# Corrections and outputs share one PSUM bank, state products take the other, and the work around them is spread: one layer of a hybrid attention and recurrence backbone

## The chip, the cores and the metric

The kernel runs on one core of a Trainium2 chip. A core has a matrix engine (TensorE, PE in the profile; PEld are its weight loads), a vector engine (VectorE, DVE), a scalar engine (ScalarE, ACT), GpSimd (POOL), a queue that issues transfers (SyncE, SP) and 16 DMA engines. Matmul results land in PSUM, which has 8 banks of 512 fp32 values in each of 128 partitions; DVE and ACT empty it. The metric is the time of one execution on the device, in microseconds; lower is better.

## The reference, cut to what matters

One layer works on 1024 latent tokens and 256 context tokens of width 1024. One input projection feeds 8 heads of differential attention and 16 heads of a recurrence that is run in both directions; both are gated and go through one output projection, and a norm ends it.

```python
def rwkv_scan(r, w, k, v, kk, b, s0, reverse):
    def step(S, inp):
        r_t, w_t, k_t, v_t, kk_t, b_t = inp
        sa = jnp.einsum('bhvk,bhk->bhv', S, -kk_t)
        S = S * w_t[:, :, None, :] + sa[..., None] * b_t[:, :, None, :] + v_t[..., None] * k_t[:, :, None, :]
        return S, jnp.einsum('bhvk,bhk->bhv', S, r_t)
    s_final, y = lax.scan(step, s0.astype(F32), xs, reverse=reverse)

def block(qblk):                                        # attention, 128 queries
    s = jnp.einsum('bqhmd,bkhmd->bhmqk', qblk, k).astype(F32) * scale
    p = jax.nn.softmax(s, axis=-1)
    a = p[:, :, 0] - lam * p[:, :, 1]
    return jnp.einsum('bhqk,bkhv->bqhv', a.astype(v.dtype), v)
```

After the scan the outputs of both directions are added, normed for each head, given a bonus and a gate, and projected together with the attention.

## The kernel before, in words

The first part of the kernel norms the tokens and makes all projections; it is not changed. For the recurrence, it cuts time into chunks of 32 steps and writes the operands of each chunk to DRAM: `ra` (receptance and removal keys) and `kt` (key rows, and the triangular products inside a chunk). A triangular 32x32 system has to be inverted for each chunk; `inverse` does this on GpSimd for a whole item at a time and writes the result to DRAM as `td`.

The second part, `mix_phase`, interleaves recurrence, attention, norms and output projection. The recurrence works on groups of four pairs of heads. An item is one group over 256 tokens (8 chunks); there are 10 items. A tick is one chunk of an item, with both directions and all 8 heads of the group at once, so there are 80 ticks. A part is two ticks (`HN`), and the operands `L` and `R` of a part lie in one of two slots, which `load_part` fills a part ahead. The four pairs are handled as two pair groups (`duos`, index `w`).

`step` writes the instructions of a tick in this order. Corrections: 32 small matmuls (line 893) give the part of the update that depends on the state. They are copied from PSUM into the rows 96 to 127 of `R` (line 901), for one pair group by ACT and for the other by DVE. In the second tick of a part, `prep` multiplies the next part's `L` with the inverse `Tb` (line 803) into the PSUM tile `yb`, and ACT copies that into `L` (line 806). State products: 32 matmuls (line 913) give the new state; DVE multiplies them with the decay of the chunk into the next `R` (line 924). Outputs: 32 matmuls (line 936), copied by ACT into the tile `ys` (line 939), which `store_y` writes to DRAM. Each pair group has a bank of PSUM of its own, `bank[w]`, in which corrections, outputs and state products of this pair group lie beside each other. The framework lets two engines on one bank follow the order of the text, also where they touch different columns.

Two calls of `fill` in a tick put other work into the text: pieces of `attention` by a credit in units of the kernel's own cost table (`RATES` and `total`), pieces of the inversion of the next item, and steps of the generators in `norms` and `projs`. Attention works on blocks of 128 queries: `scores` (line 1057 on PE, line 1060 on DVE, then the exponential on ACT, line 1068), `weight` and `combine` on DVE, `trans` (line 1089 on PE, line 1091 on ACT), `values` (line 1104). `norm` norms the recurrence's outputs of two pairs over 256 tokens; `load_wo` loads and splits the output weights into a high and a low part (`wst`, `wohi`, `wolo`).

The text's order is not yet the engines' order. A planner gives each instruction a priority by its place in the text and lays out for each engine, ahead of the run, a fixed sequence: at each point the ready instruction with the best priority, by the planner's own estimate of durations. `ahead(n)` moves the priority of a stretch of text `n` places forward; `HPC` is 500. On the chip each engine and SP's queue then take their instructions strictly in that sequence, each waiting for its own semaphores.

## Time and profile before

| what | value |
|---|---|
| runs, median of 3 | 2613.61 us (2607.57 to 2620.56) |
| profiled execution | 2612.43 us |
| its span, first to last instruction | 2610.6 us |
| mean granted clock of TensorE, share of full speed | 0.943 |
| projections | 0 to about 1240 us |
| recurrence with attention | about 1240 to 2390 us |
| tail | to the end |

The span is the time from the first to the last instruction of the profiled execution. An engine's busy time is the union of its instructions; matmuls are pipelined, so a busy PE need not be at its peak. The granted clock is the share of full speed that PE's clock was given. A wait is put down to the instruction that released it.

### The profile page before, as it was taken

The page shows a single profiled execution, that of the slowest core. Times are in us where ns is not written, and L with a number is a line of the kernel's source. Part 1 is how long each engine was busy: PE and PEld are TensorE (multiplying, and loading weights), DVE is VectorE, ACT ScalarE, POOL GpSimd, SP SyncE. Part 2 cuts the span into 40 slices and gives each one's busy share as a digit, 9 for nine tenths or more (in the row PEclk, how much of TensorE's full clock was granted, in tenths as well). Part 3 has the DMA queues.
Part 4 walks back from the last instruction along what each step waited for, and adds up shares of the span by engine and source line. Part 5 has one row for each costly group of instructions (what it writes and reads, how often), then busy time and mean ns, then how long its engine had stood idle before and what let it go on. Part 6 is the DMA issues. An engine that isn't in the chain of part 4 may idle for free.

```text
span 2610.6 us, 60873 instructions
## 1 busy us (share of the span) xinstructions
PE 2363.7 (91%) x23907; PEld 1902.6 (73%) x23907; DVE 1559.8 (60%) x3210; ACT 1192.9 (46%) x2606; POOL 1166.5 (45%) x1725
## 2 busy tenths in 40 slices
PE   6999999999999999898698989898989998898796
PEld 4888888888888888787466767676766676776674
DVE  5656565555455655533566877685745565576558
ACT  3334443334334343331466666574545554564342
POOL 4234343243433342465446666556647311043564
PEclk9999999999999999998799999897988998999898
DMA  7465656565646564567978887877887888787445
GB/s 240 108 157 134 178 143 181 139 164 161 155 128 161 135 180 120 165 167 165 225 156 166 163 163 146 165 150 169 167 200 183 211 191 190 176 222 207 148 146 181
DMA packets 516734, 437.56 MB, mean 168 GB/s; under 512 B 156552, under 2 KB 460852, under 8 KB 511329
## 3 DMA queue, kind: packets, MB, share of 16 engines
q1 hardware_dynamic: 514352, 427.94, 66.8%
q0 software_dynamic: 2096, 5.75, 1.2%
q8 instruction: 188, 3.08, 0.5%
q14 instruction: 98, 0.79, 0.1%
HBM read 258.69 MB, written 163.86 MB: 162 GB/s over the span
## 4 chain that ended last, share of the span: by engine, by line
PE 55%; DMA 19%; DVE 8%; POOL 6%; SPq 5%; issue 3%; ACT 2%; POOLq 0%; DVEq 0%; ACTq 0%
DMA L<-kt 5%; PE sc L1057 5%; PE po L1104 4%; PE bank L913 3%; PE pa L1089 3%; PE yb L803 3%; PE pg L449 3%; DMA acc<-acc 2%; PE pso L1298 2%; DMA wst<-w_out 2%; PE pso L1299 1%; DMA Tb<-td 1%; PE pso L1300 1%; PE bank L936 1%; PE psg_v L335 1%
## 5 line engine op out<-in xcount | busy, mean ns | idle before, releaser
L1057 PE MATMUL sc<-ka,q 128*128 128x512 f32 (+1 forms) x832 | 302.3, 452 | 17.5 <-DVE pb L1060 9.3
L1060 DVE TENSOR_SCALAR_CACHE_REDUCE pb<-sc,mn 128x512 f32<-128x512 f32 x256 | 191.6, 749 | 112.2 <-PE sc L1057 104.4
L1068 ACT ACTIVATE pb<-pb,mn 128x1536 f32<-128x1536 f32 (+1 forms) x160 | 218.4, 1365 | 75.3 <-DVE pb L1060 74.5
L734 POOL TENSOR_TENSOR tmp<-aw,tt 128x31 f32<-128x31 f32 (+15 forms) x310 | 163.4, 527 | 168.9 <-DMA aw<-kt 67.8
L1104 PE MATMUL po<-vk,aT 128*128 128x128 f32 x1600 | 237.2, 289 | 0.9 <-ACT aT L1091 0.7
L1104 PEld LDWEIGHTS po<-vk,aT 128*128 128x128 f32 x1600 | 217.2, 201 | 17.2 <-ACT aT L1091 1.4
L479 POOL TENSOR_SCALAR ta<-ta,ka 128x256 f32<-128x256 f32 x80 | 81.1, 1014 | 292.8 <-DVE bk L477 292.7
L456 ACT COPY km<-ptk 64x256 f32<-64x256 f32 x320 | 117.4, 367 | 182.3 <-PE ptk L453 160.4
L736 POOL TENSOR_TENSOR tt<-tt,tmp 128x31 f32<-128x31 f32 (+15 forms) x310 | 180.8, 583 | 18.2
L803 PE MATMUL yb<-L,Tb 32*32 32x96 f32 x2496 | 105.3, 269 | 81.1 <-DMA L<-kt 59.5
L806 ACT COPY L<-yb 32x384 f32<-32x384 f32 x312 | 146.3, 469 | 67.9 <-PE yb L803 63.8
L1057 PEld LDWEIGHTS sc<-ka,q 128*128 128x128 f32 x832 | 137.8, 201 | 53.6 <-DVE pb L1060 20.1
L1081 DVE SCALAR_TENSOR_TENSOR pb<-pb,cc,pb 128x512 f32<-128x512 f32 (+1 forms) x208 | 167.8, 856 | 2.0
L1091 ACT COPY aT<-pa 128x512 f32<-128x512 f32 (+1 forms) x208 | 116.2, 570 | 104.0 <-PE pa L1089 102.2
L924 DVE TENSOR_TENSOR R<-bank,wc 64x256 f32<-64x256 f32 x312 | 130.9, 420 | 54.6 <-PE bank L913 45.3
L450 DVE TENSOR_TENSOR km<-pg,msk 128x512 f32<-128x512 f32 x80 | 55.1, 688 | 175.7 <-PE pg L449 147.0
L1089 PE MATMUL pa<-ident,pb 128*128 128x128 f32 x800 | 137.7, 297 | 17.6 <-DVE acc L1292 10.4
L803 PEld LDWEIGHTS yb<-L,Tb 32*32 32x32 f32 x2496 | 66.3, 114 | 116.2 <-issue 42.2
L1060 DVE TENSOR_SCALAR_CACHE_REDUCE pb<-sc 128x512 f32<-128x512 f32 (+1 forms) x160 | 101.3, 636 | 80.7 <-PE sc L1057 67.8
L913 PEld LDWEIGHTS bank<-R,L 128*64 128x64 f32 x2560 | 102.2, 152 | 49.1 <-issue 20.5
L913 PE MATMUL bank<-R,L 128*64 128x64 f32 x2560 | 126.2, 244 | 8.3 <-ACT R L901 4.3
L1089 PEld LDWEIGHTS pa<-ident,pb 128*128 128x128 f32 x800 | 97.2, 150 | 45.1 <-DVE acc L1292 13.1
(354 smaller groups left out, 6496.2 us busy)
## 6 DMA issues: line engine op xcount, KB each, us to landing
kt<-km SPq DMA_DIRECT2D x160, 256.0 KB
L<-kt SPq DMA_DIRECT2D x80, 512.0 KB
acc<-acc SPq DMA_DIRECT2D x50, 512.0 KB
ra<-ra SPq DMA_DIRECT2D x160, 128.0 KB
L<-ra SPq DMA_DIRECT2D x80, 256.0 KB
R<-vb SPq DMA_DIRECT2D x160, 64.0 KB
y<-ys SPq DMA_DIRECT2D x80, 128.0 KB
yn<-y SPq DMA_DIRECT2D x40, 256.0 KB
```

The costliest lines, as they stand in the source:

```text
L734: e.tensor_tensor(mv, aw[:n, t, t + 1:CH].unsqueeze(2).broadcast_to([n, w, j]), tt[:n, t:t + 1, 0:j].broadcast_to([n, w, j]), op=ALU.mult)
L736: e.tensor_tensor(tt[:n, t + 1:CH, 0:j], tt[:n, t + 1:CH, 0:j], mv, op=ALU.add)
L803: nc.tensor.matmul(pp[32 * q:32 * q + 32, n:n + 96], Tb[96:128, e, HN * q + c, :], L[96:128, e, q // 2, q % 2, c, 0:96], start=True, stop= ...
L806: nc.scalar.copy(L[96:128, :, q // 2, q % 2, :, 0:96], pp[32 * q:32 * q + 32, 0:192 * HN].rearrange("p (e c y) -> p e c y", e=2, y=96))
L913: nc.tensor.matmul(bank[w][hv(h), o_:o_ + 64], L[:, e, h, d, k, 0:64], R[:, k, d, e, hv(h)], start=True, stop=True, tile_position=(0, 64 * h))
L924: nc.vector.tensor_tensor(dst[:, :, :, hv(h)], bank[w][hv(h), 256:512].rearrange("p (d e v) -> p d e v", e=2, d=2), wcs[p0][hv(h), 2 * w:2 ...
L1057: nc.tensor.matmul(sc, q[:, v, m, qc], ka[:, m, 0:kn], start=(v == 0), stop=(v == 1))
L1060: nc.vector.tensor_scalar(pm[:, c * 512:c * 512 + kn], sc, -0.125, mn[:, c - 1:c] if c else None, op0=ALU.mult, op1=ALU.min, accum_out=mn[ ...
L1068: nc.scalar.activation(v, v, AF.Exp, bias=mn[:, c:c + 1], scale=-1.0, accum_out=B["l"][:, m, B["b"]:B["b"] + 1])
L1081: nc.vector.scalar_tensor_tensor(a, B["p"][1][:, v], B["cc"], a, op0=ALU.mult, op1=ALU.add)
L1089: nc.tensor.transpose(pt[:, t * P:(t + 1) * P], B["p"][0][:, 512 * c + t * P:512 * c + (t + 1) * P], ident)
L1104: nc.tensor.matmul(po, B["aT"][c][:, t * P:(t + 1) * P], vk[:, t, :], start=(c == 0 and t == 0), stop=(c == last and t == nt - 1))
```

## The change

The two PSUM tiles change their roles. `bank[0]` takes the corrections (columns 0 to 255) and the outputs (256 to 511) of both pair groups, `bank[1]` their state products. The corrections are emptied in four copies of 32x256, all on ACT, for eight of 32x128 on two engines; the outputs in one copy for two. All of the tick from the corrections to the multiplies, the first `prep` included, is put ahead by 500 places (before, only copies and multiplies were); the outputs are put ahead by `HPY`, which is 0. An output tile holds two chunks for four, in two buffers for one, and is stored once a part.

The inversions run as one generator over all items. It is paced evenly at 33 steps for each 8 ticks and starts 4 ticks ahead (`INVA`), where before it ran at 8 steps a tick from the start of each item. In `norm`, one add and two subtracts go from GpSimd to DVE. In `attention`, exponentials are written one or two pieces later than their scores, `weight` and `combine` of a block move into the next block's text, one at a time, and the values stand between scores. The credit starts at minus two ticks (`LEAD`). `load_wo` issues two loads ahead of the split of the first.

```diff
--- before.py
+++ after.py
@@ -33,6 +33,8 @@
 CH = 32
 SEG = 256
 NC = SEG // CH
+INVA = 4
+LEAD = 2
 HN = 2
 NF = NC // HN
 NL = 4
@@ -45,7 +47,7 @@
 RATES = (1.06, 0.68)
 ES = 1
 TBUF = 1
-YBUF = 1
+YBUF = 2
 NDEL = 10
 ODEL = 14
 PDEL = 2
@@ -833,7 +835,7 @@
...
-    bank = [psx.tile([P, 512], F32, name=f"bank{w}") for w in duos]
+    bank = [psx.tile([P, 512], F32, name=f"bank{n}") for n in range(2)]
     yb = psx.tile([P, 512], F32, name="yb")
     sts, wcs = {}, {}
 
@@ -859,7 +861,7 @@
             nc.gpsimd.memset(R[0:64, 0], 0.0)
         if sg != 0:
             return
-        px = bank[w]
+        px = bank[1]
...
@@ -884,35 +886,34 @@
         c = HN * f + k
         p0, sg = items[m]
         hv = lambda h: slice(64 * h, 64 * h + 64)
-        for w in duos:
-            L, R = slots[w, j % 2]
+        later_prep = k == HN - 1 and j + 1 < n_part
+        with ahead(HPC):
             for d in range(2):
                 for e in range(2):
-                    for h in range(2):
-                        u = 64 * e + 32 * h
-                        nc.tensor.matmul(bank[w][u:u + 32, 64 * d:64 * d + 64], L[0:96, e, h, d, k, 96:128],
-                                         R[0:96, k, d, e, hv(h)], start=True, stop=True, tile_position=(0, u))
+                    for w in duos:
+                        L, R = slots[w, j % 2]
+                        for h in range(2):
+                            u, o_ = 64 * w + 32 * h, 128 * d + 64 * e
+                            nc.tensor.matmul(bank[0][u:u + 32, o_:o_ + 64], L[0:96, e, h, d, k, 96:128],
+                                                 R[0:96, k, d, e, hv(h)], start=True, stop=True, tile_position=(0, u))
+            for w in duos:
+                R = slots[w, j % 2][1]
+                for h in range(2):
+                    u = 64 * w + 32 * h
+                    nc.scalar.copy(R[96:128, k, :, :, hv(h)],
+                                   bank[0][u:u + 32, 0:256].rearrange("p (d e v) -> p d e v", d=2, e=2))
+            if later_prep:
+                prep(j + 1, 0, yb)
+        fill(0)
         with ahead(HPC):
             for w in duos:
-                R = slots[w, j % 2][1]
+                L, R = slots[w, j % 2]
                 for e in range(2):
-                    for h in range(2):
-                        u = 64 * e + 32 * h
-                        (nc.vector.tensor_copy if w else nc.scalar.copy)(
-                            R[96:128, k, :, e, hv(h)], bank[w][u:u + 32, 0:128].rearrange("p (d v) -> p d v", d=2))
-        later_prep = k == HN - 1 and j + 1 < n_part
-        if later_prep:
-            prep(j + 1, 0, yb)
-        fill(0)
-        for w in duos:
-            L, R = slots[w, j % 2]
-            for e in range(2):
-                for d in range(2):
-                    for h in range(2):
-                        o_ = 256 + 128 * d + 64 * e
-                        nc.tensor.matmul(bank[w][hv(h), o_:o_ + 64], L[:, e, h, d, k, 0:64],
-                                         R[:, k, d, e, hv(h)], start=True, stop=True, tile_position=(0, 64 * h))
-        with ahead(HPC):
+                    for d in range(2):
+                        for h in range(2):
+                            o_ = 256 * w + 128 * d + 64 * e
+                            nc.tensor.matmul(bank[1][hv(h), o_:o_ + 64], L[:, e, h, d, k, 0:64],
+                                                 R[:, k, d, e, hv(h)], start=True, stop=True, tile_position=(0, 64 * h))
             for w in duos:
                 if k < HN - 1:
                     dst = slots[w, j % 2][1][0:64, k + 1]
@@ -921,24 +922,24 @@
                 else:
                     dst = slots[w, (j + 1) % 2][1][0:64, 0]
                 for h in range(2):
-                    nc.vector.tensor_tensor(dst[:, :, :, hv(h)], bank[w][hv(h), 256:512].rearrange("p (d e v) -> p d e v", e=2, d=2),
-                                            wcs[p0][hv(h), 2 * w:2 * w + 2, sg + 1, :, c:c + 1].rearrange("p e d o -> p d e o").broadcast_to([HD, 2, 2, HD]), op=ALU.mult)
-        g = c // 4
-        if c % 4 == 0:
-            ysb[m, g] = cp.tile([P, 4, NL, HD], F32, tag="ys", name=f"ys{m}_{g}", bufs=YBUF)
-        for w in duos:
-            L, R = slots[w, j % 2]
-            for e in range(2):
-                o_ = P + 64 * e
-                for h in range(2):
-                    for d in range(2):
-                        q = 64 * d + 32 * h
-                        nc.tensor.matmul(bank[w][q:q + 32, o_:o_ + 64], L[:, e, h, d, k, 64:96], R[:, k, d, e, hv(h)],
-                                         start=True, stop=True, tile_position=(0, q))
-        for w in duos:
-            nc.scalar.copy(ysb[m, g][:, c % 4, 2 * w:2 * w + 2], bank[w][:, P:2 * P].rearrange("p (e v) -> p e v", e=2))
-        if later_prep:
-            prep(j + 1, 1, yb)
+                    nc.vector.tensor_tensor(dst[:, :, :, hv(h)], bank[1][hv(h), 256 * w:256 * w + 256].rearrange("p (d e v) -> p d e v", e=2, d=2),
+                                                 wcs[p0][hv(h), 2 * w:2 * w + 2, sg + 1, :, c:c + 1].rearrange("p e d o -> p d e o").broadcast_to([HD, 2, 2, HD]), op=ALU.mult)
+        g = c // HN
+        if k == 0:
+            ysb[m, g] = cp.tile([P, HN, NL, HD], F32, tag="ys", name=f"ys{m}_{g}", bufs=YBUF)
+        with ahead(HPY):
+            for w in duos:
+                L, R = slots[w, j % 2]
+                for e in range(2):
+                    o_ = 256 + P * w + 64 * e
+                    for h in range(2):
+                        for d in range(2):
+                            q = 64 * d + 32 * h
+                            nc.tensor.matmul(bank[0][q:q + 32, o_:o_ + 64], L[:, e, h, d, k, 64:96], R[:, k, d, e, hv(h)],
+                                             start=True, stop=True, tile_position=(0, q))
+            nc.scalar.copy(ysb[m, g][:, k], bank[0][:, 256:512].rearrange("p (x v) -> p x v", x=NL))
+            if later_prep:
+                prep(j + 1, 1, yb)
         fill(1)
 
     def store_y(m, g):
@@ -949,7 +950,7 @@
...
-                dst = (dst[:, ::-1] if d else dst)[:, 4 * g:4 * g + 4]
+                dst = (dst[:, ::-1] if d else dst)[:, HN * g:HN * g + HN]
...
@@ -973,18 +974,16 @@
         y = [y[:, :, d] for d in range(2)]
...
-        yield
-        yield
+        for _ in range(4):
+            yield
...
-        nc.gpsimd.tensor_tensor(y[0], y[0], y[1], op=ALU.add)
-        yield
-        yield
+        nc.vector.tensor_tensor(y[0], y[0], y[1], op=ALU.add)
         nc.vector.tensor_reduce(m, v4(y[0]), op=ALU.add, axis=AX.X)
         nc.vector.tensor_scalar(m, m, 1.0 / HD, None, op0=ALU.mult)
         for t in range(2):
             mean = m[:, t].rearrange("p (h x) -> p h x", x=2).unsqueeze(3).broadcast_to([P, 2, 2, HD])
-            nc.gpsimd.tensor_tensor(y[1][:, t].rearrange("p (x h v) -> p h x v", x=2, v=HD), y[0][:, t].rearrange("p (h x v) -> p h x v", x=2, v=HD), mean,
+            nc.vector.tensor_tensor(y[1][:, t].rearrange("p (x h v) -> p h x v", x=2, v=HD), y[0][:, t].rearrange("p (h x v) -> p h x v", x=2, v=HD), mean,
                                     op=ALU.subtract)
         yield
         yield
@@ -1043,6 +1042,7 @@
     def attention():
         blocks = [(h, qb) for h in range(heads) for qb in (FORD if h == heads - 1 else range(NT))]
         st = {}
+        soon, late = [], []
 
         def scores(n, m, c):
             h, qb = blocks[n]
@@ -1061,11 +1061,9 @@
                                     op1=ALU.min, accum_out=mn[:, c:c + 1])
             if c < nk - 1:
                 return
-            w = kn * nk
-            ns = 1 if nk == 1 else ES
-            for k in range(ns):
-                v = pm[:, w // ns * k:w // ns * (k + 1)]
-                nc.scalar.activation(v, v, AF.Exp, bias=mn[:, c:c + 1], scale=-1.0, accum_out=B["l"][:, m, B["b"]:B["b"] + 1])
+            v = pm[:, 0:kn * nk]
+            soon.append(lambda: nc.scalar.activation(v, v, AF.Exp, bias=mn[:, c:c + 1], scale=-1.0,
+                                                     accum_out=B["l"][:, m, B["b"]:B["b"] + 1]))
 
         def weight(n):
             h, qb = blocks[n]
...
-            vp = []
-            if pp is not None:
-                vp = [(pp, c) for c in range(1 if len(st[pp]["ch"]) > 1 else 0, len(st[pp]["ch"]))]
-
-            def old_values():
-                if vp:
-                    values(*vp.pop(0))
-
-            for c in range(nk):
-                scores(n, 0, c)
-                yield cost
-                if c < nk - 1 and vp:
-                    old_values()
-                    yield 0.87
-            while vp:
-                old_values()
-                yield 0.87
+            cb = list(range(kp_))
+
+            def item(f, r, *a):
+                f(*a)
+                if late:
+                    late.pop(0)()
+                late.extend(soon)
+                soon.clear()
+                return r
+
+            vq = [(pp, c) for c in range(len(st[pp]["ch"]))] if pp is not None else []
+            for c in range(max(nk, len(vq))):
+                if c < nk:
+                    yield item(scores, cost, n, 0, c)
+                if c == 2 and cb:
+                    combine(p, cb.pop(0))
+                if c < len(vq):
+                    yield item(values, 0.87, *vq[c])
+                if c == 1 and cb:
+                    weight(p)
+                    combine(p, cb.pop(0))
+            if len(cb) == kp_ and cb:
+                weight(p)
+            while len(cb) > (1 if kp_ == 3 and nk == 3 else 0):
+                combine(p, cb.pop(0))
             for c in range(max(nk, kp_)):
+                if c < nk:
+                    yield item(scores, cost, n, 1, c)
+                if cb:
+                    combine(p, cb.pop(0))
                 if c < kp_:
-                    trans(p, c)
-                    yield 0.43
-                if c < nk:
-                    scores(n, 1, c)
-                    yield cost
-            if new:
-                weight(n)
-                for c in range(nk):
-                    combine(n, c)
-            if kp_ > 1:
-                values(p, 0)
-                yield 0.87
+                    yield item(trans, 0.43, p, c)
+            if not new:
+                while late:
+                    late.pop(0)()
...
@@ -1240,17 +1242,27 @@
     n_set = (heads + 1) // 2
 
     def load_wo(nm, sl, whi, wlo, ks, g=None):
+        got = []
+
+        def split():
+            w, k, c = got.pop(0)
+            if g is not None:
+                nc.gpsimd.tensor_tensor(w, w, g[:, c], op=ALU.mult)
+            nc.scalar.copy(whi[:, k, c], w)
+            nc.gpsimd.tensor_tensor(wlo[:, k, c], w, whi[:, k, c], op=ALU.subtract)
+
         for k in ks:
             for n in range(2):
+                if len(got) == 2:
+                    split()
                 c = slice(n * 512, n * 512 + 512)
                 w = op.tile([P, 512], F32, tag="wst", name=f"wst{nm}_{k}_{n}", bufs=2)
                 nc.sync.dma_start(w, i["w_out"][0, sl[k]:sl[k] + P, c])
-                if g is not None:
-                    nc.gpsimd.tensor_tensor(w, w, g[:, c], op=ALU.mult)
-                nc.scalar.copy(whi[:, k, c], w)
-                nc.gpsimd.tensor_tensor(wlo[:, k, c], w, whi[:, k, c], op=ALU.subtract)
-                if n:
-                    yield
+                got.append((w, k, c))
+                yield
+        while got:
+            split()
+        yield
 
     def project(j):
         sl = [h * P for h in (2 * j, 2 * j + 1) if h < heads]
@@ -1411,13 +1423,20 @@
                     break
                 turn(outs)
                 state["credit"] -= r
-            if state["inv"] is not None:
-                for _ in range(2):
-                    next(state["inv"], None)
+            while state["ninv"] < 33 * (state["t"] + INVA + _ / 4 + pos / 2) / NC:
+                next(state["inv"], None)
+                state["ninv"] += 1
             turn(norms)
             turn(norms, 1)
             turn(projs)
 
+    def inverses():
+        for b in range(1, n_item):
+            yield from invert(b)
+            yield
+
+    state["inv"], state["ninv"] = inverses(), 0
+    state["credit"] = -LEAD * total / n_tick
     for t in range(n_tick):
         m, c = t // NC, t % NC
         p0, sg = items[m]
@@ -1428,16 +1447,14 @@
         if c == 0:
             for w in duos:
                 start_item(w, m)
-            if m + 1 < n_item:
-                state["inv"] = invert(m + 1)
             if sg == 2 and m + 2 < n_item:
                 load_pairs(m + 2)
         if 1 <= j and j + 1 < n_part:
             if k == 0:
                 load_part(j + 1)
         step(j, k, fill)
-        if c % 4 == 3:
-            at(t + 1, lambda m=m, g=c // 4: store_y(m, g))
+        if k == HN - 1:
+            at(t + 1, lambda m=m, g=c // HN: store_y(m, g))
         if c < NC - 1:
             continue
         for sg_, gs in ((-1, (8,)), (2, (2, 4)), (3, (0, 6))):
```

## Rows read from the trace of the kernel before

**Rows 1.** The page: the span, and the chain that ended last, by engine and line.

```profile
span 2610.6 us, 60873 instructions
...
PE 55%; DMA 19%; DVE 8%; POOL 6%; SPq 5%; issue 3%; ACT 2%; POOLq 0%; DVEq 0%; ACTq 0%
DMA L<-kt 5%; PE sc L1057 5%; PE po L1104 4%; PE bank L913 3%; PE pa L1089 3%; PE yb L803 3%; PE pg L449 3%; DMA acc<-acc 2%; PE pso L1298 2%; DMA wst<-w_out 2%; PE pso L1299 1%; DMA Tb<-td 1%; PE pso L1300 1%; PE bank L936 1%; PE psg_v L335 1%
```

**Rows 2.** Busy time of each engine (instructions), granted clock, DMA share, GB/s by stage.

```profile
1240.00:2390.00 1150.00, 1011.77 (x13787) 772.86 (x13786) 742.91 (x1872) 657.15 (x1573) 555.30 (x998) 0.91 0.82 179
2390.00:2611.00 221.00, 173.72 (x832) 134.66 (x830) 144.09 (x289) 76.83 (x162) 116.53 (x145) 0.91 0.51 169
...
1240.00:1300.00 60.00, 37.53 (x579) 27.05 (x578) 29.03 (x73) 21.36 (x52) 21.92 (x40) 0.74 1.03 229
```

**Rows 3.** The corrections' line: count, ns min/median/max, first and last start.

```profile
L893 PE MATMUL bank<-R,L x2560: 216/219/317, 1242.9 to 2379.8; 96*32 96x64 f32 x197
```

**Rows 4.** Timeline of one tick, then of two rows of another: start, us, engine, line.

```profile
1599.81 0.35 PE L893 MATMUL bank<-R,L 96*32 96x64 f32 x12
...
1601.21 1.06 ACT L901 COPY R<-bank 32x128 f32<-32x128 f32 x4
...
1602.89 1.20 PE L913 MATMUL bank<-R,L 128*64 128x64 f32 x32
...
1605.27 1.74 DVE L924 TENSOR_TENSOR R<-bank,wc 64x256 f32<-64x256 f32 x4
...
1607.06 0.43 PE L936 MATMUL bank<-R,L 128*32 128x64 f32 x16 [0.22 <-DVE R L924]
...
1608.14 0.44 ACT L939 COPY ys<-bank 128x128 f32<-128x128 f32 x2
...
1610.13 0.32 PE L893 MATMUL bank<-R,L 96*32 96x64 f32 x8
...
1423.94 0.69 PE L913 MATMUL bank<-R,L 128*64 128x64 f32 x16
...
1424.74 0.85 DVE L924 TENSOR_TENSOR R<-bank,wc 64x256 f32<-64x256 f32 x2
```

**Rows 5.** Waits of PE in 1235 to 2400: us in total, times, longest.

```profile
PE yb L803 <- DMA L<-kt: 59.5, 23, 10.4
PE yb L803 <- DMA Tb<-td: 15.2, 4, 8.3
...
PE sc L1057 <- DVE pb L1060: 6.3, 11, 1.5
...
PE pa L1089 <- DVE pb L1081: 5.1, 9, 1.1
```

**Rows 6.** The outputs' line 936: what ended the idle time of PE and its loads.

```profile
  DVE R L924: 19.1, 31
```

**Rows 7.** Groups of instructions by form: busy us, mean ns, idle before.

```profile
L806 ACT COPY L<-yb 32x384 f32<-32x384 f32 x312 | 146.3, 469 | 67.9 <-PE yb L803 63.8
...
L901 DVE COPY R<-bank 32x128 f32<-32x128 f32 x320 | 92.6, 289 | 44.4 <-PE bank L893 36.9 <-PE bank L936 1.4 <-ACT aT L1091 1.0
...
L901 ACT COPY R<-bank 32x128 f32<-32x128 f32 x320 | 81.7, 255 | 29.5 <-PE bank L893 25.6
...
L939 ACT COPY ys<-bank 128x128 f32<-128x128 f32 x160 | 39.8, 266 | 82.8 <-PE bank L936 72.7 <-DMA y<-ys 3.5 <-issue 2.6
...
L987 POOL TENSOR_TENSOR yn<-yn,m 128x256 f32<-128x256 f32 x40 | 25.9, 669 | 9.3 <-DVE m L984 8.3 <-DVE cc L1074 0.9
L980 POOL TENSOR_TENSOR yn<-yn 128x512 f32<-128x512 f32 x20 | 25.8, 1291 | 65.7 <-DMA yn<-y 54.0 <-DVE pb L1060 10.5 <-PE sc L1057 1.2
```

**Rows 8.** The stores of y on SP's queue: count, ns min/median/max of one issue.

```profile
L953 SPq DMA_DIRECT2D y<-ys x80: 302/432/1717, 1292.7 to 2386.6; - x80
```

**Rows 9.** The chain in order of time, two of its three wst pieces.

```profile
1306.24 8.24 DMA wst<-w_out
...
1332.68 9.38 DMA wst<-w_out
```


## Prediction

> **What bounds the kernel now.** The page comes first: the span is 2610.6 us, and the chain of work that ended last runs 55% through TensorE (PE) and 19% through DMA, with the loads of `L` from `kt` as its largest item [rows 1]. A share over the whole span hides stages, so I cut it at the recurrence. The first 1240 us (projections) are not touched by the change. The recurrence stage lasts from 1240 to 2390 and the tail to 2611 [rows 2]. In the stage PE is busy 1011.8 of 1150 us: 138 us idle. The granted clock there is 0.91, so of 1150 us some (1 - 0.91) x 1150 = 104 us of full-speed work are lost. The clock has two levels (1.2 and 2.4 GHz), and it stands lower where PE idles more: 0.74 in the first 60 us, where PE is busy only 37.5 [rows 2]. I read 104 / 138 = 0.75 us of clock lost for each idle microsecond; that is an estimate from this stage, not a law.
>
> The stage holds 80 ticks of the recurrence between 1242.9 and 2379.8 [rows 3], 14.2 us each. One tick in the timeline shows what follows what [rows 4]: the corrections on PE at 1599.81, their copies (those on ACT from 1601.21), the state products at 1602.89, the decay multiplies on DVE at 1605.27, the outputs on PE (their second half at 1607.06, after 0.22 us of waiting for those multiplies), the copy of outputs at 1608.14, the next corrections at 1610.13. Nothing in it stands free: a tick is one chain, and attention fills PE between its links. What PE waits for in the stage is mostly none of these links but the `prep` products, which wait for loads: 59.5 us on `L`, 23 times, and 15.2 us on `Tb` [rows 5]. So three things make the stage: PE's own work, the waits of `prep` (some 75 of 138 us idle), and the chain (most of the remaining 63).
>
> **The change, part by part.** All sums go against this execution: 2612.4 us, of which 1.8 lie around the span; the median of the runs is 2613.6, so the two agree.
>
> *Banks.* Outputs now go to the corrections' bank, which the decay multiplies don't read, so PE need not wait for them: the wait removed is 19.1 us, 31 times, over PE and its weight loads [rows 6]. Some of it will be taken by the next link; I take -15 (0 to -19). Behind that, the multiplies (1.74 us for four) and the outputs with their copy can run side by side where now they follow each other: up to 1.7 us a tick, 139 us in 80 ticks. But a shorter chain can only give back idle PE time, and of the 63 us left after `prep`, 15 are counted. I take a third of the other 48: -16 (0 to -48).
>
> *Four copies.* Now 320 copies of 32x128 run on ACT (255 ns) and 320 on DVE (289 ns) [rows 7], side by side: four are 1.02 and 1.16 us a tick. Afterwards 320 of 32x256 run on ACT alone. This shape is not in the rows; between 255 ns at 128 and 469 ns at 384 columns [rows 7] it lies at 362 ns, so four take 1.45 us: some 0.25 us a tick more on the chain than DVE's four, 20 us if nothing covers it. On the other side DVE's copies no longer stand behind its long attention instructions, and no second queue has to come through. I take +5 (0 to +20). Loads of the engines: ACT gains 320 x 0.107 = 34 us and loses about 14 in the output copies (80 of 128x256 at some 0.36 for 160 at 0.266), +20 on 657 busy of 1150; DVE loses 92.6. Both have room.
>
> *Output tiles half as long, two buffers.* The stores of `y` go from 80 to 160, each half as large. At 432 ns an issue [rows 8] that is 35 us more of SP's queue, some 0.9 us a part; the bytes stay. They are issued in the text just ahead of the next part's loads, so what is queued behind them on SP is `L`, `Tb` and `R`, and who waits for those is `prep`. If each were 0.9 us later in 39 parts: +35. I take 0, since the loads are released by the outputs and the stores only by the copy after them, and keep both ends (0 to +35).
>
> *`prep` ahead.* The first `prep` and all of the chain up to the multiplies now carry the priority that only the copies and multiplies had. PE takes its instructions in a fixed order, so this can only move `prep` earlier against its load. I take 0 here, because most first preps already wait for their load; its bad end is a rival below.
>
> *Inverse spread.* The work on POOL stays; it starts four ticks earlier and ends at about the same tick. What could be late today is `Tb`: 15.2 us of PE [rows 5]. I take -8 (0 to -15).
>
> *Norm's adds.* 20 adds and 40 subtracts (25.8 and 25.9 us) leave POOL for DVE [rows 7]; at most that much, 51.7, against DVE's 92.6 less. Covered by DVE's idle third (743 of 1150 busy): 0. Without that cover it is some 0.6 us a tick.
>
> *Output weights.* The split into high and low parts moves two loads behind the load. The chain goes three times through `wst` loads between 1306 and 1342 (8.24 us the first, 9.38 the last [rows 9]); ACT and POOL wait in order for the load there, and the corrections' copies stand behind them. Late next is SP, which still waits for a free buffer. I take -10 (0 to -26, three at about 8.8).
>
> *Attention's text.* The delayed exponentials and the spread combines change which instruction stands in front of which, not their number. What they could win is PE's wait for attention on DVE, 6.3 and 5.1 us in the stage [rows 5]; what they could lose has no row, and I bound it by as much. I take 0 (-11 to +11). The credit starts two ticks lower, so 2/80 of attention, 11.5 of the 459 units (about microseconds of PE) in the kernel's own table, goes to the tail. The first ticks don't get shorter for it: in 1240 to 1300 the DMA engines are full (share 1.03) and PE waits [rows 2]. In the tail PE is busy 174 of 221 us, so it costs there: +8 (0 to +12).
>
> *Clock.* Idle time returned is 15 + 16 - 5 + 8 = 34 us; at 0.75 it brings 25 more (0 to -60): -25.
>
> Sum: -15 - 16 + 5 - 8 - 10 + 8 - 25 = -61, so 2612.4 - 61 = 2551 us. With every term at its good end it is -19 - 48 - 15 - 26 - 11 - 60 = -179 (2433), with every one at its bad end +20 + 35 + 11 + 12 = +78 (2690). Both ends at once are unlikely; the likeliest case by itself lies in 2495 to 2598.
>
> **A rule against it.** In the rows of another tick, the two pair groups run one behind the other: the first 16 state products start at 1423.94 and take 0.69, and the multiplies of that half start at 1424.74 without the second half [rows 4]. They can, since each group has a bank of its own. The Trainium skill ("PSUM — Partial Sum Buffer", section PSUM bank collisions) says that two engines must not be on one bank and quadrant at once, even at different columns, so that waits have to guard the bank. The rows agree in this: PE's outputs wait for DVE's multiplies though they touch other columns. With both groups in one bank, the multiplies of the first half stand behind all 32 state products, and the first copy behind all 32 corrections.
>
> **The rivals.**
> *The halves lose their overlap, and the gain is eaten.* Half of the state products is 0.6 us of the 1.20 in the tick shown, half of the corrections some 0.2 to 0.3, the copies 0.25: 1.1 us a tick against at most 1.7 won. Then 0.6 us a tick is won where the chain sets the pace, which is in the idle time only: the two bank terms shrink from 31 to about 11, their clock with them, and the four copies cost 20. -11 + 20 - 8 - 10 + 8 and a clock term of 0 give 2611, no change; 2595 to 2630. For it: in the first tick shown DVE came only after all 32, in the second it did not. Against it: the two groups often have a long attention instruction between them, which hides an overlap anyway.
> *`prep` in front makes PE wait (slower).* Place: the first `prep` of a part. Now 23 of 39 wait for `L`, 2.6 us each (59.5 / 23). The others are covered by attention that stands ahead of them in PE's order. With priority, and before the state products in the text, that cover can go: 16 more at 2.6 = 42 us, the clock at 0.75 another 31, and with the state products behind them the chain gains nothing: 2612 + 73 = 2685 (2630 to 2750). It decides once PE's wait on `L` passes about 95 us, where the added idle time and its clock eat the -61. For it: DMA is busy 82% of the stage [rows 2], so that faster ticks make loads no earlier. Against it: 23 waits of short mean show that preps stand close behind their loads already.
> *It does not do what it says.* The planner's order may already do most of this, so that only copies move; that falls into the first rival's time.
>
> **How the numbers follow.** I give the forecast 0.58, the lost overlap (with the last) 0.20, the earlier prep 0.22. Half a percent, 13 us, is about what a measurement of this kernel tells from no change. The forecast lies below 2600 throughout; of the lost overlap 0.03 falls there too and 0.16 within the half percent, 0.01 above. Faster 0.61, same 0.16, slower 0.23. For 8 in 10 the range reaches from 2490 to 2650: it leaves out some 0.04 below, where nearly all good ends would have to meet, and of the earlier prep the 0.16 above 2650.
>
> **What would show it.** Right: no wait of the outputs for the multiplies; the outputs starting next to the multiplies; the stage 2390 - 1240 shorter by 60 us or so, at a clock of 0.92 to 0.94; PE's wait on `L` near 60; copies of 32x256 near 0.36 us; a tail some 8 us longer. Wrong: PE's wait of `prep` on `L` above 95 us and 30 times or more; the multiplies starting 0.6 us later after the first state product; ticks at 14 us with the same idle time; stores of `y` ahead of `L` on SP.

## The result, and the profile after

| | before | after |
|---|---|---|
| median of 4 runs each | 2616.98 us | 2580.85 us (2576.9 to 2589.76) |
| profiled execution | 2612.43 us | 2589.76 us |
| its span | 2610.6 us | 2587.6 us |
| its mean granted clock | 0.943 | 0.941 |

The ratio is 0.989, with a 95% interval of 0.9859 to 0.9921: 1.1% faster, where 2.35% was forecast. It is not the quotient of the two medians, which is 0.986. The time lies in the predicted range (2490 to 2650) and on the predicted side, with just under half of the predicted gain.

The page of after, span and chain:

```profile
span 2587.6 us, 60382 instructions
...
PE 56%; DMA 18%; DVE 7%; POOL 6%; SPq 6%; issue 3%; ACT 3%; POOLq 0%; DVEq 0%; ACTq 0%
PE sc L1057 5%; PE po L1102 5%; DMA L<-kt 5%; DMA Tb<-td 3%; PE pg L451 3%; PE yb L805 3%; PE pa L1087 3%; PE bank L915 3%; DMA acc<-acc 2%; PE bank L938 2%; PE ptk L455 2%; PE psg_v L338 1%; PE psg_v L336 1%; PE psg_v L337 1%; PE pso L1310 1%
```

The shares hardly move against [rows 1], but for two: `Tb` is 3% of the chain for 1%, and `wst`, 2% before, is no longer among the largest. The last outputs of the recurrence end at 2337 in after and at 2383 in before. Cut there, the windows of after (columns as in [rows 2]):

```profile
1240.00:2337.00 1097.00, 965.40 (x13670) 756.81 (x13670) 650.76 (x1550) 668.42 (x1462) 519.84 (x932) 0.91 0.82 183
2337.00:2588.00 251.00, 199.84 (x974) 157.77 (x963) 162.05 (x350) 92.58 (x195) 118.53 (x150) 0.90 0.52 172
```

and the same cut of before:

```profile
1240.00:2383.00 1143.00, 1006.03 (x13760) 768.78 (x13758) 735.91 (x1860) 653.59 (x1567) 550.34 (x993) 0.90 0.82 179
2383.00:2611.00 228.00, 179.45 (x860) 138.74 (x856) 151.09 (x303) 80.39 (x169) 121.49 (x149) 0.92 0.51 170
```

The stage is 46 us shorter, the tail 23 us longer. In the stage PE's busy time falls by 1006.0 - 965.4 = 40.6 us and its idle time only from 137.0 to 131.6. In the tail 20.4 us of busy PE are added and 2.6 of idle. So 20 us were only moved (behind the recurrence stand 106 scores for 86 and 240 matmuls of values for 200), and the net gain of 23 us is 20 us less busy time of PE and 3 us less idle. The prediction had it the other way round.

PE's waits in after from 1235 to 2400 (us in total, times, longest), beside [rows 5]; this takes in 63 us of the tail, where most of the waits of `sc` and `pa` lie:

```profile
PE yb L805 <- DMA L<-kt: 52.2, 16, 13.5
PE yb L805 <- DMA Tb<-td: 36.8, 14, 7.3
PE sc L1057 <- DVE pb L1060: 10.2, 11, 3.4
PE pa L1087 <- DVE acc L1304: 10.0, 4, 5.3
...
PE bank L915 <- ACT R L903: 6.9, 9, 3.0
...
PE bank L897 <- ACT ys L940: 3.0, 6, 1.3
```

The outputs' wait for the multiplies [rows 6] is gone. Of the 19.1 us that were counted there, PE's matmuls had 6.8 in 11 waits (the line of before below), and its weight loads the rest:

```profile
PEld bank L936 <- DVE R L924: 12.3, 20, 3.1
```

`L` fell from 59.5 to 52.2, `Tb` rose from 15.2 to 36.8: together 14 us more. Groups by form of after (as [rows 7]):

```profile
L903 ACT COPY R<-bank 32x256 f32<-32x256 f32 x320 | 115.9, 362 | 36.0 <-PE bank L897 28.7
L940 ACT COPY ys<-bank 128x256 f32<-128x256 f32 x80 | 29.6, 370 | 54.7 <-PE bank L938 54.0
L897 PE MATMUL bank<-R,L 96*32 96x64 f32 x2560 | 60.6, 228 | 5.7 <-ACT ys L940 3.0 <-DVE R L925 1.9
L915 PE MATMUL bank<-R,L 128*64 128x64 f32 x2560 | 116.4, 235 | 7.6 <-ACT R L903 6.9
L805 PE MATMUL yb<-L,Tb 32*32 32x96 f32 x2496 | 95.5, 273 | 98.3 <-DMA L<-kt 52.2 <-DMA Tb<-td 36.8 <-issue 5.1
L938 PE MATMUL bank<-R,L 128*32 128x64 f32 x2560 | 76.1, 235 | 0.0
L1251 ACT CAST wohi<-wst 128x512 fp32r<-128x512 f32 x32 | 19.5, 618 | 34.4 <-DMA wst<-w_out 31.9 <-PE pso L1312 2.4
```

and the same lines in before:

```profile
L893 PE MATMUL bank<-R,L 96*32 96x64 f32 x2560 | 72.8, 233 | 7.0 <-ACT ys L939 6.1 <-issue 0.9
L913 PE MATMUL bank<-R,L 128*64 128x64 f32 x2560 | 126.2, 244 | 8.3 <-ACT R L901 4.3 <-DVE R L901 3.6
L803 PE MATMUL yb<-L,Tb 32*32 32x96 f32 x2496 | 105.3, 269 | 81.1 <-DMA L<-kt 59.5 <-DMA Tb<-td 15.2 <-DMA y<-ys 3.4
L936 PE MATMUL bank<-R,L 128*32 128x64 f32 x2560 | 72.8, 235 | 7.0 <-DVE R L924 6.8
L1250 ACT CAST wohi<-wst 128x512 fp32r<-128x512 f32 x32 | 19.4, 618 | 21.4 <-DMA wst<-w_out 19.6 <-PE pso L1300 1.7
```

The same counts of the same matmuls, with nearly the same mean of one, keep PE busy for 12.2, 9.8 and 9.8 us less (corrections, state products, `prep`) and 3.3 more (outputs). Counted in the two traces, the corrections stand in 166 unbroken groups on PE in before and in 86 in after (80 would be one a tick), the state products in 165 and 124, `prep` in 163 and 127. All of PE after 1235 us falls into 2608 groups before, a group being matmuls of one line in a row, and 2414 after. Lines overlap at a group's edge, so the lines' 28 us are more than the 20 by which the union of all fell; counted from each matmul to the start of the next, 15 of these 20 us lie in the four products.

The idle time before them adds up in the same lines: corrections, state products and outputs had 7.0 + 8.3 + 7.0 = 22.3 us and have 5.7 + 7.6 + 0.0 = 13.3; `prep` had 81.1 and has 98.3.

One tick in the timeline of after (start, us, engine, line):

```profile
1603.63 0.65 PE L897 MATMUL bank<-R,L 96*32 96x64 f32 x32
1605.04 1.52 ACT L903 COPY R<-bank 32x256 f32<-32x256 f32 x4
...
1605.74 0.78 PE L915 MATMUL bank<-R,L 128*64 128x64 f32 x16
...
1606.88 0.33 PE L915 MATMUL bank<-R,L 128*64 128x64 f32 x2
...
1607.57 0.68 PE L915 MATMUL bank<-R,L 128*64 128x64 f32 x14
...
1608.18 0.32 PE L938 MATMUL bank<-R,L 128*32 128x64 f32 x8
1608.36 1.72 DVE L925 TENSOR_TENSOR R<-bank,wc 64x256 f32<-64x256 f32 x4
```

Outputs and multiplies now run side by side, and the multiplies come only after all 32 state products. Over the 78 ticks that have multiplies, they start before the last state product has ended in none of after and in 64 of before; from the first state product to the first multiply the median is 2.1 us for 1.8. But the state products are less broken up, and so the last multiply ends sooner: 3.8 us after the first state product for 5.1, and 7.4 us after the first correction for 9.8. From there to the next tick's first correction PE takes longer, 4.7 us for 3.3. A tick takes 13.7 us for 14.3 in the mean.

### The profile page after: what moved, and what is told of

The parts are those of the page before. It is cut to its first block, busy times and chain, and to the rows that moved or that the text cites. A ratio compares the mean times of both kernels' runs of the same rounds, so it can differ in the third digit from the quotient of the medians.

```text
span 2587.6 us, 60382 instructions
## 1 busy us (share of the span) xinstructions
PE 2343.8 (91%) x23907; PEld 1909.0 (74%) x23907; DVE 1486.0 (57%) x2950; ACT 1220.4 (47%) x2528; POOL 1133.3 (44%) x1665
## 4 chain that ended last, share of the span: by engine, by line
PE 56%; DMA 18%; DVE 7%; POOL 6%; SPq 6%; issue 3%; ACT 3%; POOLq 0%; DVEq 0%; ACTq 0%
PE sc L1057 5%; PE po L1102 5%; DMA L<-kt 5%; DMA Tb<-td 3%; PE pg L451 3%; PE yb L805 3%; PE pa L1087 3%; PE bank L915 3%; DMA acc<-acc 2%; PE bank L938 2%; PE ptk L455 2%; PE psg_v L338 1%; PE psg_v L336 1%; PE psg_v L337 1%; PE pso L1310 1%
## 5 line engine op out<-in xcount | busy, mean ns | idle before, releaser
L1102 PE MATMUL po<-vk,aT 128*128 128x128 f32 x1600 | 230.6, 286 | 2.9 <-ACT aT L1089 1.7
L1102 PEld LDWEIGHTS po<-vk,aT 128*128 128x128 f32 x1600 | 212.5, 199 | 19.2 <-ACT aT L1089 4.0
L738 POOL TENSOR_TENSOR tt<-tt,tmp 128x31 f32<-128x31 f32 (+15 forms) x310 | 184.1, 594 | 19.6
L805 PE MATMUL yb<-L,Tb 32*32 32x96 f32 x2496 | 95.5, 273 | 98.3 <-DMA L<-kt 52.2
L1087 PE MATMUL pa<-ident,pb 128*128 128x128 f32 x800 | 135.7, 296 | 16.7 <-DVE acc L1304 13.0
L1294 POOL TENSOR_TENSOR olo<-of,ohi 128x512 fp32r<-128x512 f32 x30 | 39.2, 1306 | 218.1 <-ACT ohi L1293 186.0
L903 ACT COPY R<-bank 32x256 f32<-32x256 f32 x320 | 115.9, 362 | 36.0 <-PE bank L897 28.7
```

The costliest lines, as they stand in the source:

```text
L738: e.tensor_tensor(tt[:n, t + 1:CH, 0:j], tt[:n, t + 1:CH, 0:j], mv, op=ALU.add)
L805: nc.tensor.matmul(pp[32 * q:32 * q + 32, n:n + 96], Tb[96:128, e, HN * q + c, :], L[96:128, e, q // 2, q % 2, c, 0:96], start=True, stop= ...
L1087: nc.tensor.transpose(pt[:, t * P:(t + 1) * P], B["p"][0][:, 512 * c + t * P:512 * c + (t + 1) * P], ident)
L1102: nc.tensor.matmul(po, B["aT"][c][:, t * P:(t + 1) * P], vk[:, t, :], start=(c == 0 and t == 0), stop=(c == last and t == nt - 1))
```

## Experiments

Four theories, each with a number that tells it apart. A: the whole gain is made in the tick (banks, copies, priority), by fewer broken groups on PE. B: it is made by the spacing of the rest (inverse, norm, weights, attention). D: each part is worth what its removal loses, so that the parts add up to 1.1%. C: any edit of the text makes the planner lay out another fixed order, and a time drawn from a scatter as large as these parts comes with it, whatever the edit. Ratios are to the kernel before, run on the same chip (its median beside the first four runs is 2603.37 us and not 2616.98, so expectations in us are read as ratios to 2616.98). PE's total busy time and groups are from each trace.

### The tick alone, and all but the tick

The first is the kernel before with the diff's part for `bank`, `step` and `store_y`; the second is after with the tick of before and the short output tiles.

```diff
# e1_step_only: before, with
-    bank = [psx.tile([P, 512], F32, name=f"bank{w}") for w in duos]
+    bank = [psx.tile([P, 512], F32, name=f"bank{n}") for n in range(2)]
... (step as in after; YBUF = 2, store each part)
# e2_old_step: after, with the reverse
```

> The kernel before with the change of the tick alone: banks, four copies, the priority, the output tiles. Inverse, attention's text, norm, output weights and credit stay as before. Theory A (the gain is longer runs of small matmuls on PE: 28 us less busy time of corrections, state products and prep, the rest of the change moves work and wins nothing): 2580 to 2595 us, corrections in 80 to 100 runs where before there were 166, PE busy some 20 to 30 us less. Theory B (the gain is the spacing of attention, inverse and weights, the tick alone is worth nothing): 2605 to 2625 us.

> The changed kernel with the tick as before: a bank for each pair group, eight copies, priority for copies and multiplies alone; output tiles, inverse, attention's text, norm, weights and credit as changed. Theory A: 2605 to 2625 us, the runs of corrections back at about 160 and PE busy back at 2360 or more. Theory B: 2575 to 2595 us.

| | us | ratio | PE busy | groups | corrections' |
|---|---|---|---|---|---|
| before | 2603.37 | 1 | 2363.7 | 2608 | 166 |
| tick alone | 2596.81 | 0.9965 (0.9938 to 0.9993) | 2350.8 | 2439 | 90 |
| all but the tick | 2603.48 | 1.000 (0.9971 to 1.003) | 2364.2 | 2650 | 199 |

The groups go with the tick, as A has it. The time does not follow: 0.35% for the tick and nothing for the rest make 0.35, not 1.1. Read as ratios, the tick alone lies where B had it, and all but the tick where A had it: each theory has one of the two times against it.

### The tick's priority, and the attention's late start

```diff
# e3_prio_old: after, with only copies and multiplies ahead
-        with ahead(HPC):
+        with ahead(0):
             for d in range(2):
... (HPC for the copies; prep after them without; 0 for the state products; HPC for the multiplies)
# e4_lead0
-LEAD = 2
+LEAD = 0
```

> The changed kernel with the priority of before (copies and multiplies alone are put ahead; corrections, the first prep and state products stand at their place in the text). Banks and four copies stay. If theory A holds because of the priority: 2605 to 2620 us, runs split again. If it holds because one bank ties both pair groups together: 2575 to 2590 us, corrections still in some 80 to 100 runs. Theory B: 2575 to 2590 us as well, with no word on the runs.

> The changed kernel with LEAD = 0, so that attention's credit starts at zero. If the tail's growth by 22 us comes from the two ticks' worth of attention (11.5 units) and costs what it saves: the tail 10 to 12 us shorter, the recurrence as much longer, 2575 to 2590 us. If attention costs nothing in the recurrence (rival): 2565 to 2575 us. If the first ticks are what is won by the lead: 2590 to 2605 us.

With the old priority: 2586.64 us, 0.9941 (0.9914 to 0.9968). The corrections are broken again (151 groups) and the outputs less (109 for 152); all groups together are 2479, PE is busy 2345.4 us. So the runs split again, as A had it with the priority as cause, and the time, read as a ratio, lies between A's two cases. With `LEAD` at 0: 2595.42 us, 0.9972 (0.9948 to 0.9995); the recurrence ends at 2369.7, and the tail is 231.3 us for 250.3. The shift to the tail goes with `LEAD`: 19 us less of it, more than the 10 to 12 expected. Read as a ratio, the time lies above all three ranges, nearest to the third. The run is 0.8% slower than after; the section on two numbers below shows how little that says of `LEAD`.

### After again, and three other parts undone

```diff
# e5_after: no edit
# e6_old_att: after, with the attention's text of before (scores, values, weight, combine in the old order)
# e7_old_inv: after, with
-            while state["ninv"] < 33 * (state["t"] + INVA + _ / 4 + pos / 2) / NC:
-                next(state["inv"], None)
-                state["ninv"] += 1
+            if state["inv"] is not None:
+                for _ in range(2):
+                    next(state["inv"], None)
... (invert(m + 1) set at each item's start, as before)
# e8_old_wo_norm: after, with norm and load_wo of before
```

> The changed kernel itself, beside the three that follow, so that they are compared on one chip: about 0.989 of the kernel before (0.986 to 0.992).

> The changed kernel with attention's text as before (exponentials right behind their scores, weight and combine at the end of their own block, values late); LEAD stays 2. If the spaced text is what the tick needs to win (the tick alone gave 0.35%, the tick beside the rest 1.1%): 0.995 to 1.000 of the kernel before, with more idle time of PE in the recurrence. If the text only moves work: 0.986 to 0.992.

> The changed kernel with the inverse as before (eight steps a tick from the start of each item). If the even spread matters: 0.994 to 1.000, PE's wait on Tb rising over 37 us. If not: 0.986 to 0.992. In the changed kernel PE's wait on Tb rose from 15 to 37 us, so this may even come out faster: 0.983 to 0.987.

> The changed kernel with load_wo and norm as before (split right behind each load, the add and the subtracts on GpSimd). If ACT's wait for the loads of the output weights held up the corrections' copies: 0.992 to 0.997. If that wait was covered: 0.986 to 0.992. After the change ACT's wait for these loads is 32 us where before it was 20, so no gain is expected from it.

| | us | ratio | lost against 0.989 |
|---|---|---|---|
| after | 2575.93 | 0.9891 (0.9856 to 0.9925) | |
| attention's text undone | 2596.97 | 0.9975 (0.9946 to 1.0005) | 0.85% |
| inverse undone | 2582.51 | 0.9923 (0.9893 to 0.9954) | 0.3% |
| norm and weights undone | 2599.95 | 0.998 (0.9949 to 1.0011) | 0.9% |

The time of after is a property of its text: 0.989 came out a second time. With the whole tick undone (1.1%) and `LEAD` (0.8), the five parts that together are the change lose 1.1 + 0.8 + 0.85 + 0.3 + 0.9 = 3.95%, of a whole of 1.1. D can't hold unless nearly every part needs all the others; C says simply that after is a good draw. Of the single expectations, the attention's fell in the range of "needs the spaced text", though idle time in the recurrence hardly rose (135.7 us for 131.6 and 133.4); the inverse fell between its ranges, with no rise of the wait on `Tb`; norm and weights lost more than either of theirs.

These traces do tell one mechanism. PE's waits of `prep` with the tick of after and the old inverse (e7):

```profile
PE yb L805 <- DMA L<-kt: 50.1, 18, 8.9
PE yb L805 <- DMA Tb<-td: 34.6, 13, 9.2
```

and with the old tick and the new inverse (e2):

```profile
PE yb L805 <- DMA L<-kt: 58.6, 26, 6.2
PE yb L805 <- DMA Tb<-td: 9.2, 3, 6.3
```

So the wait on `Tb` rose with the tick and not with the inverse. In all profiles it is 9 to 24 us with the old tick (9.2, 12.2 and 20.2 with the new inverse, 14.9 to 24.1 with the old) and 29.5 to 43 with the new one. The priority of `prep` isn't what does it: with the old priority (e3) it is 48.2 us, and there `L` is down to 12.5. What the traces do show is the time that the load has. `Tb` has one buffer, and its load is issued in no part before the last `prep` of the part before has ended. From this issue to the next part's first `prep` the median is 12.1 to 14.9 us in the eight profiles with the old tick, 7.5 to 10.8 in the eleven with the new one and 7.0 in e3; over all 20 profiles it goes with the wait on `Tb` at a correlation of -0.90. So the new tick, in which the first `prep` comes sooner, leaves the load less time. A second buffer for `Tb` was not tried.

### Two numbers that have nothing to do with the change

`ODEL` and `NDEL` say how many turns the projection's transposes, and the norm's, are held back in the text. One more or less adds no work and takes none away; it shifts a few instructions in the text. If D or A held alone, before and after should stay put, one some 1.1% below the other.

```diff
# e9_after_odel, e11_before_odel
-ODEL = 14
+ODEL = 13
# e10_after_ndel, e12_before_ndel
-NDEL = 10
+NDEL = 9
# e13_before_odel15, e14_after_odel15, e17_old_step_odel15 (on e2): ODEL = 15
# e15_before_ndel11, e16_after_ndel11, e18_old_step_ndel11 (on e2): NDEL = 11
```

> The changed kernel with ODEL = 13 for 14: the transposes of attention's outputs stand one turn earlier in the text, four small products for each head. No work and no stage depends on it. Theory C (each edit of the text reshuffles the engines' fixed orders, and the times scatter by 0.3 to 0.8% whatever the edit; undoing a part of the change costs this scatter, not what the part was worth): 0.992 to 1.000 of the kernel before. Theory D (each part undone was worth what its run lost, 0.8 to 1.1%): an edit that means nothing costs nothing, 0.986 to 0.992.

> The changed kernel with NDEL = 9 for 10: the transposes of norm stand one turn earlier in the text. Theory C: 0.992 to 1.000 of the kernel before. Theory D: 0.986 to 0.992.

> The kernel before with ODEL = 13 for 14. Theory C: anywhere in 0.993 to 1.007, most likely over 1.000, since the text of before has been settled with its own numbers. Theory D: 0.998 to 1.002.

> The kernel before with NDEL = 9 for 10. Theory C: anywhere in 0.993 to 1.007. Theory D: 0.998 to 1.002.

> The kernel before with ODEL = 15 for 14. Scatter theory: 0.992 to 1.010, drawn around 1.001, the mean of the three texts of before so far. PE busy in all 2345 to 2380 us.

> The changed kernel with ODEL = 15 for 14. If the change is worth about 0.6% below the scatter (its three texts have a mean of 0.995): 0.985 to 1.004. If it is worth the measured 1.1%: 0.986 to 0.992. If it is worth nothing: around 1.001. PE busy in all 2320 to 2345 us, corrections in 85 to 95 runs.

> The kernel before with NDEL = 11 for 10. Scatter theory: 0.992 to 1.010. PE busy in all 2345 to 2380 us.

> The changed kernel with NDEL = 11 for 10. If the change is worth about 0.6% below the scatter: 0.985 to 1.004. If it is worth the measured 1.1%: 0.986 to 0.992. If nothing: around 1.001. PE busy in all 2320 to 2345 us.

> The changed kernel with the tick as before, and ODEL = 15 for 14. If the tick (banks, copies, priority) carries the worth of the change: around 1.001 like the texts of before (0.992 to 1.010), PE busy in all 2350 to 2380 us. If the rest carries it: around 0.995, like the texts of the changed kernel.

> The changed kernel with the tick as before, and NDEL = 11 for 10. If the tick carries the worth: around 1.001 (0.992 to 1.010), PE busy in all 2350 to 2380 us. If the rest carries it: around 0.995.

| ratio (95% interval) | before's text | after's text | before - after |
|---|---|---|---|
| as it is | 1 | 0.989 (0.9859 to 0.9921) | 1.1% |
| `ODEL` 13 | 1.008 (1.005 to 1.0111) | 1.0032 (1.0006 to 1.0059) | 0.48 |
| `NDEL` 9 | 0.9962 (0.9926 to 0.9999) | 0.9928 (0.9905 to 0.995) | 0.34 |
| `ODEL` 15 | 0.990 (0.9867 to 0.9932) | 0.9959 (0.9934 to 0.9984) | -0.59 |
| `NDEL` 11 | 1.0025 (0.9993 to 1.0056) | 0.9936 (0.9907 to 0.9965) | 0.89 |

After with the old tick gave 0.996 (0.993 to 0.9989) with `ODEL` 15 and 0.9946 (0.9923 to 0.9969) with `NDEL` 11, for 1.000 without.

Of the eight complete texts with a shifted number, five lie in the ranges that the scatter theory gave them; 1.0032, 1.008 and 0.990 lie even outside them, so the scatter is wider than expected. PE's busy time lies in its range in all six runs that were given one. With the old tick, 0.996 and 0.9946 are nearer to "the rest carries it" and 1.000 to "the tick carries it": not decided.

One number takes 1.4% from after (0.989 to 1.0032, 2610.69 us) or gives before 1.0% (2576.78 us, as fast as the whole change). C holds. Over the five pairs the change is worth 0.44% in the mean, with a standard deviation of 0.65; 2.78 x 0.65 / sqrt(5) makes its 95% interval 0.44 +- 0.81: not told from zero. Wider, with all texts of this study: ten with the new tick average 0.9956 (deviation 0.0039), eight with the old 0.9984 (0.0055); 0.28% between them, +- 0.5. (These are not independent drawings; five of the ten lack a part, and the old priority on the new banks, 0.9941, is in neither.)

What the draw changes can be read in the windows. After with `ODEL` 13, then before with `ODEL` 15, from 1240 to 2610:

```profile
1240.00:2610.00 1370.00, 1164.64 (x14560) 908.39 (x14559) 816.45 (x1897) 760.76 (x1653) 635.72 (x1082) 0.90 0.74 176
```

```profile
1240.00:2610.00 1370.00, 1177.88 (x14571) 896.32 (x14560) 880.11 (x2156) 734.79 (x1731) 675.96 (x1141) 0.92 0.76 176
```

and their waits on loads, in the same order:

```profile
PE yb L805 <- DMA L<-kt: 50.1, 15, 11.6
PE yb L805 <- DMA Tb<-td: 34.9, 15, 5.7
```

```profile
PE yb L803 <- DMA L<-kt: 31.5, 11, 8.6
PE yb L803 <- DMA Tb<-td: 14.9, 6, 5.2
```

Before with `ODEL` 15 has the busier PE and is 34 us faster: in its stage PE idles 110 us for 147, with 46 us of waits on `L` and `Tb` for 85, and the clock is 0.92 for 0.90. Within before's text, from `ODEL` 14 to 15, the idle time and these waits fall together (137.0 to 109.7 us, 74.7 to 46.4). But within after's text, from 14 to 13, the idle time rises from 131.6 to 147.0 us while these waits fall from 89.0 to 85.0. So late loads are one place where a draw is decided and not the only one; that it hangs on which instruction stands in front of a late load is argued, not shown.

What depends less on the draw is PE's busy time. In the 11 profiles with the new tick it is 2337 us in the mean (2321 to 2351), in the eight with the old 2363 (2347 to 2379), at the same mean clock in the stage (0.909 and 0.907): 26 us, or 1.0%, less. Their groups on PE number 2407 and 2630; 26 / 223 = 0.12 us for each group more. The old priority on the new banks lies between in both: 129 groups fewer than before and 18 us less. That the broken groups cause all of it isn't shown: counted from each matmul to the start of the next, of the 24.5 us that fall after 1235, 12 lie in the tick's four products and the other 12.5 in the rest, attention's matmuls above all. And the spans differ by 12 us only (2590.6 and 2602.6), so 14 of the 26 us come back as idle time; in the stage the new tick idles 137 us in the mean for 129. The waits on the loads give as much: `Tb` 36.0 us in the mean for 17.2, `L` 43.3 for 47.4, together 15 us more.

## Why the prediction was wrong

The step that failed is the one that carried the sum: **idle time returned**, 34 us from banks, copies and inverse, and the **clock** of 25 us worked out from it, 59 of the 61. Measured, the stage's idle time fell by 5.4 us and the clock went from 0.904 to 0.905: the tick's three products returned 9.0 us where the banks were to return 31, and `prep` took 17.2 where the inverse was to return 8. The gain came from a term that the prediction didn't have: PE itself is busy 20 us less, with its small matmuls in fewer groups (15 of the 20 us lie in the tick's products; that the breaks cause it is argued). That the sign came out right was luck in this sense.

*Banks (-15 and -16).* The wait removed was removed, all of it. But the term was too large from the start: 19.1 us is the idle time of PE and of its weight loads added up, and PE's own, which the 138 us of idle are counted in, was 6.8. The state products wait nearly as before (7.6 us for 8.3), and `prep` waits 14 us more for its loads. The third of the idle that a shorter chain was to give back did not come, although the chain did get shorter: from the first correction to the end of the last multiply by 2.4 us in the median. More than half of this, 1.4 us, goes to a longer pause before the next corrections. The lost overlap of the first rival, which the prediction had named, came in every tick (0 of 78), but its cost did not, since the last multiply ends 1.3 us sooner and not later. The Trainium skill ("PSUM — Partial Sum Buffer", section PSUM bank collisions raise a hardware error) wants two engines kept apart by bank and quadrant, and not by columns; the trace of after agrees: no multiply starts while state products of the other pair group are still written to the shared bank. The rival's 2611 left out PE's busy time, as the forecast did; without it, its sum of -1 us is near the 3 us less idle that were measured, though by other terms.

*Copies (+5).* The duration was right: 362 ns estimated, 362 measured, 370 for the output copy (0.36). Four of them are 1.45 us against 1.16, so 0.29 us a tick more and not 0.25. What they cost on the path was not separated.

*`prep` ahead (0), inverse (-8).* With the old tick the new inverse takes some 5 of the 8 us (9.2 to 20.2 us of wait on `Tb` in three profiles, 13.9 in the mean, for 14.9 to 24.1 in five with the old inverse, 19.2 in the mean; the ranges overlap). But the new tick adds more than that, whichever the inverse (34.6 us with the old one, 36.8 with the new), because it leaves the load of `Tb` less time. The waits on both loads rose by 14.3 us (74.7 to 89.0), a third of the 42 us that the second rival put on `L` alone; `L` itself fell from 59.5 to 52.2, in 16 waits and not over 30. The rival named the right place, `prep` in front of its loads, but the wrong load, and not the priority as the reason (e3).

*Stores of `y` (0).* Right: 160 stores, and no wait of PE's matmuls for them in after (3.4 us before); its weight loads wait 7.0 us for them, 12.4 before.

*Norm's adds (0).* Not separated: e8 undoes them together with the output weights.

*Output weights (-10).* Wrong sign in its own place: ACT waits 31.9 us for `wst`, for 19.6 us before. With the old code in after (e8) it is 27.5, so the reordering removes none of it. The chain's pieces on `wst` between 1300 and 1360 did shrink, from 23.1 us to 9.8, but with the old code in after they are 11.4 as well.

*Attention's text and `LEAD` (+8).* The tail grew by 23 us and not by 8, but 20 of these are work that the stage no longer has. In idle time it cost 2.6. Counting the added tail without the shortened stage was wrong; undoing it (e4) gave no gain.

*Clock (-25).* That idle time buys clock at 0.75 us each was read from one execution. Two profiles of after, with 131.6 and 133.4 us of idle in the stage, show 0.905 and 0.920. Over all 20 profiles of this study idle time and clock go together only weakly (correlation -0.36). A whole term of 25 us can't stand on this.

*What no term held.* The time of this kernel moves by -1.0 to +0.8% in before, and by +0.4 to +1.4% in after, with a number that does no work. A prediction by parts, most of them below 0.6%, can't be tested on one text. The measured 1.1% is true of this text and repeats; what the change is worth apart from its text it doesn't tell.

Still open: whether the change is worth anything beyond the scatter (0.44 +- 0.81%), the worth of each of its parts, and which few places of the order set the idle time of a draw. No run was clearly faster than after: before with `ODEL` 15 (0.990) and after (0.989) can't be told apart.

## What to carry to other kernels

Where a planner fixes the order of every engine from the text, first shift something that does no work, in both kernels, and see how far the time moves: below that, a single before and after tells nothing of a part's worth. Look at the busy time too, not only at the waits: here the tick with fewer broken groups went with 1% less busy time of PE. A wait that is removed helps only as far as nothing else waits in its place: here the waits for loads took back more (14 us) than the shorter chain returned (9). And before a wait is priced, take apart what an engine's matmuls and its weight loads waited. A term for the clock needs more than one execution to rest on.

## What the runs showed of the hardware

Two things were not expected. Each change between groups of matmuls on PE went with some 0.12 us of busy time (26 us for 223 groups, between the means of two families of kernels; inside a family the relation is weak, so it is a mean price and not a cause shown by itself; half of the 26 us lie in matmuls outside the tick). And the granted clock of the same program's stage differs by 1.5 points between two executions with nearly the same idle time: `after` has 0.905 in its stage (0.91 in the window shown above), and its second profile, of the run e5, has 0.920:

```profile
1240.00:2324.00 1084.00, 950.65 (x13649) 744.96 (x13648) 645.89 (x1550) 667.23 (x1461) 517.03 (x932) 0.92 0.83 184
```

With it, the busy time of the same program differs by 18 us in all (2343.8 and 2325.9 us) and the span by 12 (2587.6 and 2575.5).
